# The token norms of an input projection, moved from its input to where its chunks are emptied

## The chip, the cores and the metric

The kernel runs on one core of one Trainium2 chip. The metric is the device time of one execution in microseconds (us): the median over several runs, each on the chip. A separate execution is recorded by the hardware profiler, and all views of the profile come from that one. The engines are named as in the profile: PE is TensorE (PEld its weight loads), DVE is VectorE, ACT is ScalarE, POOL is GpSimd, SP is SyncE, whose queue issues most of the DMAs.

## The reference, cut to what matters

One layer of a streaming encoder over 16 learned meta tokens and 256 tokens of width 2048, everything in float32.

```python
h = concat([meta, x])                                  # 272 tokens x 2048
xn = rmsnorm(h, norm_mix)                              # h * rsqrt(mean(h*h) + eps) * norm_mix
q, f_logit, i_in, g_out, u = split(xn @ w_in)          # 4 x 1024 columns, and 1024 of u
o_hg = hgrn2_mixer(q, f_logit, i_in, g_out, ...)       # 8 heads; silu(q), sigmoid(f), v = i, silu(g)
o_s5 = s5_mixer(u, ...)                                # scan, GELU, GLU with w_glu, norm
h = h + concat([o_hg, o_s5]) @ w_out
h = h + conv_ffn(rmsnorm(h, norm_ffn), w_gate, w_up, conv_w, conv_b, w_down)
out = rmsnorm(h[:, 16:], final_norm)
```

The factor rsqrt(...) of a token is one number for its row of xn, so it is also one number for its row of xn @ w_in. norm_mix is one number for each of the 2048 input channels.

## The kernel before, in words

All weights stream from HBM once, in units of 1 MB (128 partitions x 2048 values, tile `raw`, three buffers). A float32 product is made of three single-pass matmuls: each operand is split into a rounded high part and the rest, and hi\*hi, hi\*lo and lo\*hi are added up in PSUM. For the weights `wsplit` does it: ACT casts a half of a unit (128x1024) to `whi`, and DVE subtracts that from `raw` into `wlo`; three buffers of each. The input of the projection is split the same way into `xh` and `xl`, sixteen K tiles of 128 channels x 272 tokens, with tokens along the free axis. `mm3` (L173) runs over the units, their halves, the two blocks of 128 columns and the four K tiles of a half, with three matmuls each (L187, L188, L189).

`chunk` (L772) computes 256 columns of w_in: two units, two accumulators `acc` of 128x272 (or 258) in the PSUM pool `pmm`, which has three buffers, and 96 matmuls. The twenty chunks run in the order written in `ORDER`: u0, then for h0 the three chunks f, q and i, then u1, h1 and so on to h3, and at the end g0 to g3. Each chunk is emptied at once:

- u: `s5_u` (L560) copies both accumulators into `ysb` on ACT. The S5 part follows (`s5_tile`, `s5_scan`): per chunk eight scans of DVE, ACT and POOL work and small matmuls.
- f: `hg_f` (L639): per accumulator two sigmoids on ACT that read PSUM.
- q and g: `hg_q` (L650) and `hg_g` (L675): a sigmoid on ACT and then a product on DVE, both reading PSUM.
- i: `hg_i` (L658): ACT copies to SBUF, PE transposes, ACT copies the transposes into `v` and `vm`.
- After f, q and i the HGRN2 work of two heads follows (`hg_group`, `hg_cross`), most of it on DVE.

After the twenty chunks come the GLU (its input is split into `gh` and `gl` at L827 and L828), the output projection, the MLP and the down projection, which are not touched.

The start is what the change rewrites. The x rows (tokens on partitions) are loaded in four halves, PE transposes them, and DVE and ACT copy the transposes to `xT` (L311 to L321). `row_rs` (L268) takes a row block's sum of squares, half on ACT (L275) and half on DVE (L276), and `sqrt_rs` (L258) makes the inverse root with five small DVE instructions and one on ACT. `spread` (L290) turns the three columns into a tile `rbs` that has each token's factor on every partition, through PE and PSUM. Ten matmuls into a spare accumulator follow (NWARM2, L305). Then each K tile takes three instructions: DVE `xn` = xT\*gm\*rbs (L333), ACT `xh` (L334), DVE `xl` (L335). The first chunk's two weight units are loaded early (`early`, L247 and L251) and split in halves of 512 columns, where DVE makes the `wlo` of the first quarter of a unit and POOL the other three; one-column copies from `xh` (L160, `deps`) hold these splits back behind certain K tiles.

The instructions are ordered by a planner: each gets a priority from its place in the program, `pri(n)` moves a block forward (negative) or back, and the planner simulates the engines and takes, for each, the ready instruction with the best priority. Weight splits have -4, the emptying -3, HGRN2 work -2, the main matmuls of `mm3` +1. The whole start stands 900000 ahead of everything else. On the chip each engine then runs its instructions in the planned order. `tc.issue_after(i)` puts the instructions of its block behind instruction i on i's engine.

Of the kernel before, what the change touches and what calls it, by code (L numbers as in the profile page):

```python
# [9 lines left out]
F32 = mybir.dt.float32  # L10
# [7 lines left out]
NM = 16  # L18
# [11 lines left out]
T0 = NM - 2  # L30
# [9 lines left out]
NWARM2 = 10  # L40
# [33 lines left out]
def hymba_kernel(ctx: ExitStack, tc: tile.TileContext, x, meta, lb_logits, norm_mix, w_in, hg_norm,  # L74
# [71 lines left out]
    deps = []  # L146

    def wunit(src):
        with pri(-4):
            return wsplit(early.pop(0), (dve, pool), 2, deps.pop(0)) if early else wsplit(wload(src))  # L150

    def wsplit(raw, eng=(dve, dve), parts=1, dep=None):
        res = []
        n = 1024 // parts
        for hf in range(2):
            hi = wsp.tile([128, 1024], F32R, tag="whi", name="whi")
            lo = wsp.tile([128, 1024], F32R, tag="wlo", name="wlo")
            if dep is not None and dep[hf] is not None:

                act.copy(out=hi[:, 0:1], in_=dep[hf])  # L160
            for i in range(parts):
                c = slice(i * n, (i + 1) * n)
                act.copy(out=hi[:, c], in_=raw[:, hf, c])  # L163
                tt(lo[:, c], raw[:, hf, c], hi[:, c].bitcast(F32), SUB, eng[max(hf, i)])
            res.append((hi, lo))
        return res
# [61 lines left out]
    sp.dma_start(out=xm, in_=meta)  # L228
    HD = D // 2
# [12 lines left out]
    for b in range(2):  # L242
        for hf in range(2):
            sp.dma_start(out=xt[b][:, hf * HD:(hf + 1) * HD], in_=x[b * 128:(b + 1) * 128, hf * HD:(hf + 1) * HD])
        if b == 0:
            sp.dma_start(out=nrow, in_=norm_mix.rearrange("o (r c) -> (o r) c", c=128))
# [40 lines left out]
    rbp = [pmm.tile([128, NM + 128], F32, tag="mm", name=f"rbp{b}") for b in range(2)]  # L287
    rbs = xin.tile([128, T], F32, name="rbs")
# [5 lines left out]
    rm = row_rs(xm, NM, 1, "rm")  # L294
    rb = [None, None]
    for b in range(2):
        rb[b] = row_rs(xt[b], 128, 2, f"rb{b}")
        if b == 0:
            spread(rm, NM, rbp[0][:, 0:NM])
            spread(rb[0], 128, rbp[0][:, NM:])  # L300
            act.copy(out=rbs[:, 0:NM + 128], in_=rbp[0])
        else:
            spread(rb[1], 128, rbp[1][:, 0:128])
            dve.tensor_copy(out=rbs[:, NM + 128:T], in_=rbp[1][:, 0:128])
            for _ in range(NWARM2):  # L305
                pe.matmul(wps, ident, rbs[:, NM + 128:T], start=True, stop=True)
        for i in range(4):
            pp, tg = ((pbu, "bu"), (py, "y"), (psc, "sc"), (pbu, "bu"))[i]
            xps = pp.tile([128, 4, 128], F32, tag=tg, name="xps")
            for k in range(4):  # L310
                pe.transpose(xps[:, k], xt[b][:, (4 * i + k) * 128:(4 * i + k + 1) * 128], ident)  # L311
            dst = xT[:, 4 * i:4 * i + 4, NM + 128 * b:NM + 128 * (b + 1)]
            if i % 2:
                act.copy(out=dst, in_=xps)
            else:
                dve.tensor_copy(out=dst, in_=xps)
        if b == 0:
            xps = ptp.tile([128, KD, NM], F32, tag="tp", name="xps")
            for kt in range(KD):
                pe.transpose(xps[:, kt], xm[:, kt * 128:(kt + 1) * 128], ident[0:NM, 0:NM])  # L320
            act.copy(out=xT[:, :, 0:NM], in_=xps)  # L321
            gm = prm.tile([128, KD], F32, name="gm")
            gps = ptp.tile([128, KD], F32, tag="tp", name="gps")
            pe.transpose(gps, nrow, ident[0:KD, 0:KD])
            ts(gm, gps, -0.5, MUL)
# [4 lines left out]
    tc.cur_priority -= 900000  # L330
    for kt in range(KD):
        xn = xin.tile([128, T], F32, tag="xn", name="xn", bufs=4)
        stt(xn, xT[:, kt], gm[:, kt:kt + 1], rbs, MUL, MUL)  # L333
        act.copy(out=xh[:, kt, :], in_=xn)  # L334
# [225 lines left out]
    def s5_u(j, ps):  # L560
        pv = ps.rearrange("p (k s) -> p s k", s=2)
        act.copy(out=ysb[:, j], in_=pv)
# [87 lines left out]
    def hg_q(h0, accs):  # L650
        q = hgp.tile([128, 2, NQ], F32, tag="q", name="q")
        sg = hgp.tile([128, 2, NQ], F32, tag="sg", name="sg")
        for m in range(2):
            fact(sg[:, m], accs[m], AF.Sigmoid)
            stt(q[:, m], accs[m], lbc[:, 1, h0 + m:h0 + m + 1], sg[:, m], MUL, MUL)
        return q

    def hg_i(accs):  # L658
# [8 lines left out]
        act.copy(out=v, in_=tp)  # L667
# [393 lines left out]
```

## Time and profile before

| | |
|---|---|
| median of 3 runs | 1241.25 us (1241.08 to 1242.11) |
| the profiled execution | 1245.4 us, span 1243.6 us |
| PE busy | 1220.0 us (98%) |
| DVE busy | 878.6 us (71%) |
| ACT busy | 605.9 us (49%) |
| POOL busy | 91.1 us (7%) |

The span runs from the first to the last instruction of the profiled execution. Matmuls overlap each other in the record, so a busy PE is not a PE at its peak: how fast it goes is read from the distance between the starts of matmuls and from the granted clock (1.00 is full speed). A view of windows gives, for each stretch, its length, the busy time of each engine with its instructions in brackets, the clock, the busy share of the DMA engines and their GB/s. A row of the timeline has start, duration, engine, line, operation, output<-inputs, shapes and count, and in square brackets the engine's idle time before it and what ended that.

### The profile page before, as it was taken

The numbers are of one execution on the slowest core, as the hardware profiler recorded it, in microseconds if no ns is written. First come the engines' busy times: TensorE is split into PE (matmuls) and PEld (weight loads), VectorE is DVE, ScalarE is ACT, GpSimd is POOL, SyncE is SP. The second block draws the span as 40 slices with busy tenths as digits, with TensorE's granted clock in tenths as the row PEclk, the third lists the DMA queues.
The fourth block names the chain that finished last, engine by engine and source line by source line (L and its number), as shares of the span: only waits on it lengthen the run. The fifth ranks groups of instructions, "written<-read, shape, count | busy, mean of one in ns | idle before, by whom it ended". The sixth has DMA issues, their size and how long they took to land.

```text
span 1243.6 us, 22643 instructions
## 1 busy us (share of the span) xinstructions
PE 1220.0 (98%) x9235; PEld 1146.4 (92%) x9235; DVE 878.6 (71%) x1535; ACT 605.9 (49%) x1054; POOL 91.1 (7%) x116
## 2 busy tenths in 40 slices
PE   7999999999999999999999999999999999999997
PEld 6999998989979999999999999999999988888886
DVE  7899999999977877765656656656656644545554
ACT  6756566675645455433433433434333434444454
POOL 5221211322100000000000000000000000000000
PEclk8999999999999999999999999999999999999999
DMA  8454443334335555565555656555565645555552
GB/s 241 147 149 131 143 142 106 113 109 144 127 102 169 171 178 196 170 195 179 183 190 176 197 171 194 179 184 190 174 199 170 230 165 184 200 201 184 191 208 97
DMA packets 176295, 210.73 MB, mean 169 GB/s; under 512 B 14772, under 2 KB 168879, under 8 KB 170415
## 3 DMA queue, kind: packets, MB, share of 16 engines
q1 hardware_dynamic: 175871, 209.20, 51.8%
q8 instruction: 72, 1.18, 0.4%
q14 instruction: 32, 0.26, 0.1%
q0 software_dynamic: 320, 0.09, 0.0%
HBM read 206.05 MB, written 2.10 MB: 167 GB/s over the span
## 4 chain that ended last, share of the span: by engine, by line
PE 95%; DVE 3%; DMA 1%; issue 0%; ACT 0%; SPq 0%; DVEq 0%; ACTq 0%
PE acc L189 10%; PE acc L188 10%; PE acc L187 9%; PE ua L188 7%; PE ua L187 7%; PE ga L187 7%; PE ua L189 7%; PE ga L189 7%; PE ga L188 7%; PE d L984 6%; PE d L982 6%; PE d L983 6%; PE bu L602 1%; PE lps L731 1%; DVE wlo L85 1%; DVE xn L94 1%
## 5 line engine op out<-in xcount | busy, mean ns | idle before, releaser
L85 DVE TENSOR_TENSOR wlo<-raw,whi 128x1024 fp32r<-128x1024 f32 (+1 forms) x376 | 461.2, 1227 | 305.1 <-ACT whi L163 255.6
L163 ACT CAST whi<-raw 128x1024 fp32r<-128x1024 f32 (+1 forms) x382 | 397.8, 1042 | 517.2 <-PE ga L188 158.2
L187 PE MATMUL ga<-fh,whi 128*128 128x258 f32 x704 | 199.0, 283 | 0.5 <-DVE a L85 0.5
L189 PE MATMUL ga<-fh,wlo 128*128 128x258 f32 x704 | 198.5, 282 | 0.0
L188 PE MATMUL ua<-fl,whi 128*128 128x256 f32 x704 | 198.4, 282 | 0.0
L188 PE MATMUL ga<-fl,whi 128*128 128x258 f32 x704 | 198.1, 281 | 0.0
L189 PE MATMUL ua<-fh,wlo 128*128 128x256 f32 x704 | 197.9, 281 | 0.0
L187 PE MATMUL ua<-fh,whi 128*128 128x256 f32 x704 | 197.9, 281 | 0.0
L188 PE MATMUL acc<-xl,whi 128*128 128x272 f32 (+1 forms) x640 | 186.9, 293 | 2.3 <-DVE xl L85 2.3
L189 PE MATMUL acc<-xh,wlo 128*128 128x272 f32 (+1 forms) x640 | 184.3, 293 | 3.8 <-DVE wlo L85 3.8
L187 PE MATMUL acc<-xh,whi 128*128 128x272 f32 (+1 forms) x640 | 185.9, 294 | 0.0
L187 PEld LDWEIGHTS ga<-fh,whi 128*128 128x128 f32 x704 | 133.0, 189 | 0.7 <-DVE a L85 0.7
L188 PEld LDWEIGHTS ga<-fl,whi 128*128 128x128 f32 x704 | 133.5, 190 | 0.0
L187 PEld LDWEIGHTS ua<-fh,whi 128*128 128x128 f32 x704 | 133.1, 189 | 0.0
L189 PEld LDWEIGHTS ua<-fh,wlo 128*128 128x128 f32 x704 | 132.9, 189 | 0.0
L188 PEld LDWEIGHTS ua<-fl,whi 128*128 128x128 f32 x704 | 132.8, 189 | 0.0
L189 PEld LDWEIGHTS ga<-fh,wlo 128*128 128x128 f32 x704 | 132.6, 188 | 0.0
L982 PE MATMUL d<-whi,ah 128*128 128x512 f32 x328 | 127.7, 389 | 0.0
L188 PEld LDWEIGHTS acc<-xl,whi 128*128 128x128 f32 x640 | 121.8, 190 | 6.4 <-DVE xl L85 3.2
L983 PE MATMUL d<-whi,al 128*128 128x512 f32 x328 | 127.6, 389 | 0.0
L189 PEld LDWEIGHTS acc<-xh,wlo 128*128 128x128 f32 x640 | 120.9, 191 | 6.7 <-DVE wlo L85 4.3
L187 PEld LDWEIGHTS acc<-xh,whi 128*128 128x128 f32 x640 | 121.1, 190 | 3.3 <-issue 1.7
(381 smaller groups left out, 1840.3 us busy)
## 6 DMA issues: line engine op xcount, KB each, us to landing
raw<-in_w_ffn_gate SPq DMA_DIRECT2D x44, 1024.0 KB, 5.1
raw<-in_w_ffn_up SPq DMA_DIRECT2D x44, 1024.0 KB, 5.1
raw<-in_w_ffn_down SPq DMA_DIRECT2D x44, 1024.0 KB, 4.8
raw<-in_w_in SPq DMA_DIRECT2D x39, 1024.0 KB, 5.2
raw<-in_w_out SPq DMA_DIRECT2D x16, 1024.0 KB, 5.4
raw<-in_w_glu SPq DMA_DIRECT2D x4, 1024.0 KB, 5.2
x<-in_x SPq DMA_DIRECT2D x4, 512.0 KB, 5.9
out<-ob SPq DMA_DIRECT2D x8, 256.0 KB, 2.8
```

Of the source, the lines that this page charges most:

```text
L85: eng.tensor_tensor(out=dst, in0=a, in1=b, op=op)
L94: dve.scalar_tensor_tensor(out=dst, in0=a, scalar=s, in1=b, op0=op0, op1=op1, **kw)
L163: act.copy(out=hi[:, c], in_=raw[:, hf, c])
L187: pe.matmul(accs[m], lh, xh[:, n0:n1], start=first, stop=False)
L188: pe.matmul(accs[m], lh, xl[:, n0:n1], start=False, stop=False)
L189: pe.matmul(accs[m], ll, xh[:, n0:n1], start=False, stop=end)
L602: return pe.matmul(bus[i][:, ri], bt[h, 2 * ri + q0 // 2], R[h, q0 // 2], start=True, stop=True)
L731: pe.matmul(ps[:, i], kt[:, i], qf[:, 64 * i:64 * (i + 1)], start=True, stop=True)
L982: pe.matmul(dps[t][n], ah[:, tk], hi, start=False, stop=False, skip_group_check=True)
L983: pe.matmul(dps[t][n], al[:, tk], hi, start=False, stop=False, skip_group_check=True)
L984: pe.matmul(dps[t][n], ah[:, tk], lo, start=False, stop=end, skip_group_check=True)
```

## The change

The K tiles of the projection's input no longer contain the tokens' factors: `xh` and `xl` are the split of xT\*gm. The twenty chunks therefore come out without the tokens' factors, and these are multiplied in where a chunk is emptied.

```diff
 # the start
+    sp.dma_start(out=nrow, in_=norm_mix...)            # now right behind meta, ahead of x
-        if b == 0:
-            sp.dma_start(out=nrow, in_=norm_mix...)
...
-    def wsplit(raw, eng=(dve, dve), parts=1, dep=None):
+    def wsplit(raw):                                   # whole halves, wlo always on DVE
...
-    rbp = [pmm.tile([128, NM + 128], F32, tag="mm", name=f"rbp{b}") for b in range(2)]
-    rm = row_rs(xm, NM, 1, "rm")
+    pe.transpose(gps, nrow, ident[0:KD, 0:KD]); dve.tensor_copy(out=gm, in_=gps)
     for b in range(2):
-        rb[b] = row_rs(xt[b], 128, 2, f"rb{b}")
-        ... spread, copies into rbs, NWARM2 matmuls
         ... transposes of x and copies into xT, as before
+    last = None
+    for p in range(8):                                 # eighths of the first chunk's two units
+        u, hf, c = p // 4, p // 2 % 2, slice(512 * (p % 2), 512 * (p % 2) + 512)
+        hi, lo = units[u][hf]
+        raw = early[u][:, hf, c]
+        def split():
+            i = act.copy(out=hi[:, c], in_=raw)
+            tt(lo[:, c], raw, hi[:, c].bitcast(F32), SUB)
+            return i.ins
+        with tc.issue_after(last):                     # from p = 1 on
+            wi = split()
+        with tc.issue_after(wi):
+            for kt in (2 * p, 2 * p + 1):
+                last = act.activation(out=xh[:, kt], in_=xT[:, kt], func=AF.Identity, scale=gm[:, kt:kt + 1]).ins
+                stt(xl[:, kt], xT[:, kt], gm[:, kt:kt + 1], xh[:, kt].bitcast(F32), MUL, SUB)
+    rcol = s5p.tile([128, 3], F32, name="rcol")
+    rb = [row_rs(xt[0], 128, 2, "rb0")]
+    with pri(0.5):
+        rb += [row_rs(xt[1], 128, 2, "rb1"), row_rs(xm, NM, 1, "rm")]
+    for i, n in enumerate((128, 128, NM)):
+        ts(rcol[:n, i:i + 1], rb[i], -0.5, MUL)
-    for kt in range(KD):
-        stt(xn, xT[:, kt], gm[:, kt:kt + 1], rbs, MUL, MUL)
-        act.copy(out=xh[:, kt, :], in_=xn)
-        tt(xl[:, kt, :], xn, xh[:, kt, :].bitcast(F32), SUB)
 # the emptying of chunks
     def s5_u(j, ps):
-        act.copy(out=ysb[:, j], in_=pv)
+        tt(ysb[:, j], pv, rv, MUL)                     # rv: rbs in the same order
     def hg_f(h0, accs):
-            fact(k[:, m], accs[m], AF.Sigmoid, scale=-1.0)
-            fact(f[:, m], accs[m], AF.Sigmoid)
+            tt(f[:, m], accs[m], rbs, MUL)
+        fact(k, f, AF.Sigmoid, scale=-1.0)
+        fact(f, f, AF.Sigmoid)
     def hg_q(h0, accs):
-            fact(sg[:, m], accs[m], AF.Sigmoid)
-            stt(q[:, m], accs[m], lbc[...], sg[:, m], MUL, MUL)
+            tt(q[:, m], accs[m], rbs[:, T0:T], MUL)
+        fact(sg, q, AF.Sigmoid)
+            stt(q[:, m], q[:, m], lbc[...], sg[:, m], MUL, MUL)
     def hg_i(accs):                                    # tokens lie on partitions here
-        act.copy(out=v, in_=tp)
+        for b in range(2):
+            fact(v[... b], tp[... b], AF.Copy, scale=rcol[:, b:b + 1])
-        act.copy(out=vm, in_=tp[0:NM, 0:2])
+        fact(vm, tp[0:NM, 0:2], AF.Copy, scale=rcol[0:NM, 2:3])
     def hg_g(h0, accs):
-            fact(sg[:, m], accs[m], AF.Sigmoid)
-            stt(gs[:, h0 + m], accs[m], vcol[...], sg[:, m], MUL, MUL)
+            tt(gs[:, h0 + m], accs[m], rbs[:, T0:T], MUL)
+            fact(sg[:, m], gs[:, h0 + m], AF.Sigmoid)
+            stt(gs[:, h0 + m], gs[:, h0 + m], vcol[...], sg[:, m], MUL, MUL)
     def do_u(c):
         accs = chunk(w_in, 16 + c)
+        if c == 0:                                     # rbs is made behind the first chunk
+            rbp = pmm.tile([128, T], F32, tag="mm", name="rbp")
+            spread(rcol[0:NM, 2:3], NM, rbp[:, 0:NM])
+            for b in range(2):
+                spread(rcol[:, b:b + 1], 128, rbp[:, NM + 128 * b:NM + 128 * (b + 1)])
+            act.copy(out=rbs, in_=rbp)
```

More of the change, by code (lines that the diff above doesn't have):

```diff
@@ L39 @@
 NWARM = 8
-NWARM2 = 10
 LATE = 1.003
@@ L157, in wsplit @@
             lo = wsp.tile([128, 1024], F32R, tag="wlo", name="wlo")
[L158 to L164, printed above, removed]
+            act.copy(out=hi, in_=raw[:, hf])
+            tt(lo, raw[:, hf], hi.bitcast(F32), SUB)
             res.append((hi, lo))
@@ L228, in hymba_kernel @@
     sp.dma_start(out=xm, in_=meta)
+    sp.dma_start(out=nrow, in_=norm_mix.rearrange("o (r c) -> (o r) c", c=128))
     HD = D // 2
@@ L286, in hymba_kernel @@
         pe.matmul(wps, ident, ident, start=True, stop=True)
-    rbp = [pmm.tile([128, NM + 128], F32, tag="mm", name=f"rbp{b}") for b in range(2)]
-    rbs = xin.tile([128, T], F32, name="rbs")
+    rbs = s5p.tile([128, T], F32, name="rbs")
     def spread(r, n, ps):
         pe.matmul(ps, r.to_broadcast([n, 128]), ident[0:n, 0:n], start=True, stop=True)
-    rm = row_rs(xm, NM, 1, "rm")
-    rb = [None, None]
+    gm = prm.tile([128, KD], F32, name="gm")
+    gps = ptp.tile([128, KD], F32, tag="tp", name="gps")
+    pe.transpose(gps, nrow, ident[0:KD, 0:KD])
+    dve.tensor_copy(out=gm, in_=gps)
     for b in range(2):
-        rb[b] = row_rs(xt[b], 128, 2, f"rb{b}")
[L298 to L306, printed above, removed]
         for i in range(4):
@@ L321, in hymba_kernel @@
             act.copy(out=xT[:, :, 0:NM], in_=xps)
[L322 to L325, printed above, removed]
+    last = None
+    for p in range(8):
+        u, hf, c = p // 4, p // 2 % 2, slice(512 * (p % 2), 512 * (p % 2) + 512)
+        if p % 4 == 0:
+            units.append([])
+        if p % 2 == 0:
+            units[u].append([wsp.tile([128, 1024], F32R, tag=t, name=t) for t in ("whi", "wlo")])
+        hi, lo = units[u][hf]
[4 more added lines that the diff above has]
+            return i.ins
+        if last is None:
+            wi = split()
+        else:
+            with tc.issue_after(last):
+                wi = split()
+        with tc.issue_after(wi):
[8 more added lines that the diff above has]
+        ts(rcol[:n, i:i + 1], rb[i], -0.5, MUL)
     tc.cur_priority += 900000
     pool.memset(ones, 1.0)
-    tc.cur_priority -= 900000
-    for kt in range(KD):
-        xn = xin.tile([128, T], F32, tag="xn", name="xn", bufs=4)
-        stt(xn, xT[:, kt], gm[:, kt:kt + 1], rbs, MUL, MUL)
-        act.copy(out=xh[:, kt, :], in_=xn)
-        tt(xl[:, kt, :], xn, xh[:, kt, :].bitcast(F32), SUB)
-    tc.cur_priority += 900000
-    deps[:] = [(None, xh[:, 0, 0:1].bitcast(F32)), tuple(xh[:, i, 0:1].bitcast(F32) for i in (3, 6))]
     vps = ptp.tile([128, 100], F32, tag="tp", name="vps")
@@ L560, in s5_u @@
     def s5_u(j, ps):
-        pv = ps.rearrange("p (k s) -> p s k", s=2)
-        act.copy(out=ysb[:, j], in_=pv)
+        pv, rv = (a.rearrange("p (k s) -> p s k", s=2) for a in (ps, rbs))
+        tt(ysb[:, j], pv, rv, MUL)
     def s5_split(j):
@@ L642, in hg_f @@
         for m in range(2):
+            tt(f[:, m], accs[m], rbs, MUL)
+        fact(k, f, AF.Sigmoid, scale=-1.0)
+        fact(f, f, AF.Sigmoid)
+        for m in range(2):
             h = h0 + m
-            fact(k[:, m], accs[m], AF.Sigmoid, scale=-1.0)
-            fact(f[:, m], accs[m], AF.Sigmoid)
             fact(f[:, m], f[:, m], AF.Identity, scale=lbc[:, 1, h:h + 1], bias=lbc[:, 0, h:h + 1])
@@ L653, in hg_q @@
         for m in range(2):
-            fact(sg[:, m], accs[m], AF.Sigmoid)
-            stt(q[:, m], accs[m], lbc[:, 1, h0 + m:h0 + m + 1], sg[:, m], MUL, MUL)
+            tt(q[:, m], accs[m], rbs[:, T0:T], MUL)
+        fact(sg, q, AF.Sigmoid)
+        for m in range(2):
+            stt(q[:, m], q[:, m], lbc[:, 1, h0 + m:h0 + m + 1], sg[:, m], MUL, MUL)
         return q
```

10 lines of the change are left out of this document (5 added, 5 removed).

## The prediction, made before the changed kernel was run

> **What bounds the kernel now.** I read the page's totals, then busy times by stage, then the timeline of the start, then the waits of the stage of the twenty chunks.
>
> ```profile
> PE 1220.0 (98%) x9235; PEld 1146.4 (92%) x9235; DVE 878.6 (71%) x1535; ACT 605.9 (49%) x1054; POOL 91.1 (7%) x116
> ```
>
> ```profile
> core 0: us, PE busy (x) PEld busy (x) DVE busy (x) ACT busy (x) POOL busy (x), PEclk, DMA share, GB/s
> 13.00:21.00 8.00, 6.52 (x31) 5.66 (x31) 7.29 (x18) 6.22 (x16) 2.98 (x3) 0.57 1.13 324
> 34.00:60.00 26.00, 26.00 (x214) 26.00 (x213) 23.05 (x99) 18.64 (x37) 6.08 (x12) 1.00 0.47 139
> 60.00:345.00 285.00, 281.20 (x2452) 258.72 (x2452) 272.79 (x560) 177.93 (x471) 66.14 (x76) 0.99 0.42 130
> 370.00:1000.00 630.00, 628.87 (x5215) 625.21 (x5215) 411.15 (x620) 266.35 (x328) 0.00 (x0) 1.00 0.57 183
> ```
>
> PE is the bound, and from 370 us on it alone: DVE is busy 411 of 630 us there, and nothing of the change lies there. From 60 to 345 us both are full: PE 281.2 and DVE 272.8 of 285 us. So an instruction added to DVE in that stage is not hidden by a glance at DVE's 71%. What is left is the start:
>
> ```profile
> 21.07 0.30 PEld L187 LDWEIGHTS acc<-xh,whi 128*128 128x128 f32 x2
> 25.37 0.29 PE L187 MATMUL acc<-xh,whi 128*128 128x272 f32 x1
> 25.50 0.29 PE L188 MATMUL acc<-xl,whi 128*128 128x272 f32 x1
> 29.61 0.39 PE L188 MATMUL acc<-xl,whi 128*128 128x272 f32 x1 [1.76 <-DVE xl L85]
> 31.18 0.43 PE L189 MATMUL acc<-xh,wlo 128*128 128x272 f32 x1
> 31.41 0.43 PE L188 MATMUL acc<-xl,whi 128*128 128x272 f32 x1
> ```
>
> ```profile
> 17.00:21.00 4.00, 4.00 (x21) 0.56 1.15 325
> 21.00:24.00 3.00, 2.85 (x24) 1.00 0.80 133
> 31.00:34.00 3.00, 3.00 (x14) 0.50 0.92 316
> 21.00:34.00 13.00, 10.49 (x63) 0.87 0.64 184
> ```
>
> The first real matmul starts at 21.07 us. At full clock they start 0.126 us apart (25.37 and 25.50; over longer stretches 0.126), at half clock 0.23 us (31.18 and 31.41, the window of clock 0.50). The last row is that of the tile `acc` alone: 63 matmuls in the 13 us to 34 us, where 103 would fit. The starved PE waits for DVE, which works off `xn` and `xl`. From 34 us on PE runs without a gap. So at 34.0 us the main work done is 63 x 0.126 = 7.9 us, and **26.1 us are lost** at the start.
>
> **The change part by part: the start.** Which steps stand there now:
>
> ```profile
> 12.89 1.12 ACT L163 CAST whi<-raw 128x512 fp32r<-128x512 f32 x2
> 13.68 0.69 DVE L85 TENSOR_TENSOR wlo<-raw,whi 128x512 fp32r<-128x512 f32 x1
> 14.28 1.22 DVE L94 SCALAR_TENSOR_TENSOR rb1y<-rb1t,rb1y 128x1 f32<-128x1 f32 x1
> 17.75 1.74 DVE L94 SCALAR_TENSOR_TENSOR xn<-xT,gm,rbs 128x272 f32<-128x272 f32 x4
> 18.28 0.83 ACT L334 CAST xh<-xn 128x272 fp32r<-128x272 f32 x2 [0.45 <-DVE xn L94]
> 25.85 3.41 POOL L85 TENSOR_TENSOR wlo<-raw,whi 128x512 fp32r<-128x512 f32 x2 [2.30 <-ACT whi L163]
> 26.61 1.53 DVE L94 SCALAR_TENSOR_TENSOR xn<-xT,gm,rbs 128x272 f32<-128x272 f32 x1
> ```
>
> The first quarter of weights is there at 12.89 us (ACT casts it then). The x rows are there before (11.20, ACT's wait for the last of them; the row above it is that of the spare matmuls):
>
> ```profile
> 17.35 3.88 PE L306 MATMUL wps<-rbs,ident 128*128 128x128 f32 x19
> 11.20 0.63 ACT L82 ACTIVATE junk<-x 128x512 bf16<-128x512 f32 x1 [0.63 <-DMA x<-in_x]
> L94 DVE SCALAR_TENSOR_TENSOR junk<-x x4: 670/689/693, 6.0 to 11.7; 128x512 bf16<-128x512 f32 x4
> 8.52 3.92 SPq L142 DMA_DIRECT2D raw<-in_w_in  x2
> DMA to landing us min/median/max: 5.3/9.5/11.3
> ```
>
> Between 12.89 and 21.07 us lie the row sums, roots, `rbs`, the last transposes behind them, `gm` and `xn`. All but the transposes, their copies and `gm` leave this path. What remains: cast 0.56 us (1.12 for two), two `xh` of 0.42, so the first matmul can start at 12.9 + 0.56 + 0.42 = 13.9 us; I take 14.3 for hand-overs. If the planner leaves sums of squares ahead of the cast on ACT (four of 0.63 us), it is up to 17.
>
> Then each of the eight steps needs on DVE one `wlo` quarter of 0.62 us (0.69 less the 0.07 by which neighbours overlap in the record) and two `xl` as scalar_tensor_tensor of 0.41 (priced by `xn`: 1.74 us for four, less overlap): 1.44 us. On ACT 0.56 + 2 x 0.41 = 1.38, and on PE twelve matmuls of 0.126 = 1.51 us. So PE paces the steps, by a hair. The 16 `xn` go, and with POOL's six `wlo` goes what they did to DVE: a one-column product took 1.22 us and an `xn` 1.53 us beside POOL's. DVE takes over those six quarters (3.7 us, inside the 1.44 per step).
>
> The ten NWARM2 matmuls go, so the first matmuls meet the clock of an idle PE, 0.57 between 13 and 21 us. Bounds: none, if the transposes keep it up, or some 3.4 us at half clock (steady spare matmuls began at 17.35, and the clock is 0.56 up to 21 us and 1.00 from there), which loses 1.7 us. I take 1.6, the nearest row being that window.
>
> By the Trainium skill ("TensorE: Matmul & The Clock Gate", Part 1) PE's clock is at half by default and full after about 3.4 us of sustained activity, which would make that loss an estimated 1.7 us; the trace agrees for the way up. For the way down the page wants an idle window of about 3.4 us. There the trace differs: the wait of 1.76 us before 29.61 was followed by 0.50 from 31 to 34 us, so I price each PE wait of about 2 us at double.
>
> Lost at the start after: 14.3 + 1.6 + 0.5 for steps not met exactly = 16.4 us. **PE's lead is 26.1 - 16.4 = 9.7 us**; with a first matmul at 17 us it is 7.
>
> Costed at nothing: norm_mix's DMA ahead of x on SP's queue (one 0.43 us issue, x was waited for in 11.20 already, but 14.3 does not hang on it); the second unit's arrival, issued at 8.52 plus 9.5 = 18.0 us, against step five at 14.3 + 4 x 1.51 = 20.3; POOL's queue keeps its loads.
>
> **The emptying.** Added to DVE: 2 products per chunk of u, f, q and g, 32 in all, one operand in PSUM. The nearest row is the MLP's:
>
> ```profile
> L85 DVE TENSOR_TENSOR a<-ga,rsb x44: 416/419/426, 514.3 to 980.6; 128x258 f32<-128x258 f32 x44
> L562 ACT COPY ysb<-acc x8: 368/387/394, 41.4 to 240.5; 128x272 f32<-128x272 f32 x8
> DVE wlo L85 <- ACT whi L163: 7.7, 13, 2.4
> DVE rhv L91 <- PE hps L857: 3.1, 1, 3.1
> PE acc L189 <- DVE wlo L85: 3.8, 2, 2.1
> 345.00:364.00 19.00, 16.71 (x137) 12.97 (x135) 13.89 (x27) 9.52 (x20) 0.77 (x1) 1.00 0.32 106
> ```
>
> 32 x 0.35 to 0.42 = 11.2 to 13.4 us; I take 12. ACT loses eight copies of 0.39, merges sigmoids and gains four scalings; it has room (178 of 285 us) and is costed at nothing. The products of q and g with their sigmoids now read SBUF: same length.
>
> Does DVE hold that? From 34 to 364 us (when it splits the GLU's input) it is busy 23.05 + 272.79 + 13.89 = 309.7 of 330 us, so 20.3 idle. After: its steps run from about 13.5 for 8 x 1.44 = 11.5 us, to 25.0; of the row sums (four of 0.69, meta's of 1.2 and some 2.5 of small ones, 6.5 us) most fit into the wait before 13.5, and I leave 2 us: 27. Then 27 + 309.7 + 12 = 348.7 us plus idle time. With all 20.3 idle it ends at 369, 5 us later than now; with 6 at 354.7, which is PE's lead. 7.7 of the idle time is DVE waiting for a cast that waits for PE to free its buffer, and 3.1 waiting for PE's `hps`: both shrink when PE is ahead. Less these two it is 9.5, and I take 10.3: DVE ends at 359, **5 us earlier** than now. So of PE's lead of 9.7 us, DVE lets through 5, and what is late next is DVE's S5 work ahead of the GLU.
>
> Emptying also moves: an accumulator is now freed by one DVE product, where u and f took ACT, and q and g a sigmoid and a DVE product. `pmm` has three buffers, so the next chunk has 12 matmuls (1.5 us) before it needs one more. The first time there is no spare one, since `rbs` sits in it: row sums, three spreads, a copy and a product come before h0's first matmul. With sums done by 27 us and u0 finished at 14.3 + 1.6 + 12.1 + 0.5 = 28.5, I cost that at nothing; if all 6.5 us come after 25.0, `rbs` is there at about 33, a wait of 4 us.
>
> Sum: span 1243.6 - 5 = 1238.6 us. The profiled execution took 1245.4, 1.8 more than its span and 4.15 above the median, so against the median: 1241.25 - 5 = **1236.2 us**.
>
> **The rivals.** A: DVE absorbs all. Its idle time falls to 6 us or its S5 tail slips behind the GLU's first splits; PE's lead comes through, 1241.25 - 9.7 = 1231.6, and down to 1229.5 if the two waits for `wlo` (3.8 us, with their clock) go too. For it: most of DVE's waits are waits for a lagging PE. Against: 98% of busy time from in-order instructions is rare; it has 95.7% in the stage now.
>
> B: DVE takes it all back. With 13 to 18 us of idle time, against 20.3 now, it ends within 2.5 us of 364 (348.7 + 15.3 in the middle), and PE waits ahead of the GLU longer than now: 1241 us. For it: 12 us more of DVE work in a stage where DVE is full. This is also the case in which the change doesn't do what it says, with the start given back.
>
> C: the slower side: PE waits for its accumulators. Every chunk but i is emptied behind what DVE has in hand:
>
> ```profile
> 198.04 3.34 DVE L704 RECIPROCAL rv<-SP 128x512 f32<-128x512 f32 x1
> 202.51 0.39 PE L189 MATMUL acc<-xh,wlo 128*128 128x272 f32 x1 [1.70 <-DVE wlo L85]
> 362.80 0.51 PE L187 MATMUL acc<-gh,whi 128*128 128x258 f32 x2 [1.60 <-ACT gh L827]
> 364.21 0.39 PE L187 MATMUL acc<-gh,whi 128*128 128x258 f32 x1 [0.91 <-DVE gs L94]
> ```
>
> A reciprocal of 3.34 us outlasts the 1.5 us of cover, and did so with a `wlo`. 9.7 us spread over 16 chunks is 0.6 each: above that mean wait it decides. At 0.85 us it is 13.6 - 9.7 = 4 us slower: 1245. Against it: q and g let go after one DVE instruction instead of two in a row, and the planner places the emptying ahead of everything but splits; only one such wait (0.91) shows now.
>
> **How the numbers follow.** No change can be told from one within 0.2% (2.5 us: 1238.8 to 1243.7). Forecast 0.40 (its own range 1233 to 1238.8), A 0.25, B 0.15, C 0.20. Faster is forecast plus A, 0.65; same 0.15; slower 0.20. The range reaches from A's low end, 1229.5, to C's 1245; some 0.03 lies below and 0.12 above.
>
> **What would show it.** First real matmul at 13.9 to 17 us, with half clock for about 3 us; chunk u0 done near 28.5 instead of some 38 (34.0 and 33 more matmuls); DVE products on `acc` of 0.42 us, 32 in all; no POOL `wlo`. DVE over 96% busy between 40 and 340 us, and the GLU's first matmul near 357 instead of 362.8. The rest must keep its length. I would be wrong if `rbs` came late, if the planner set the row sums ahead of the casts, or if waits for `acc` or `wlo` multiplied in the stage.

## The result, and the profile after

The changed kernel took 1249.87 us (median of 4 runs, 1248.84 to 1250.94) against 1241.68 us for the kernel before (4 runs, 1241.08 to 1242.24): a ratio of 1.006 (95% interval 1.004 to 1.0079), 8 us slower where 5 us faster was forecast. Its profiled execution took 1250.04 us with a span of 1248.3 us, so that one stands at its median; the profiled execution of before (1245.4 us) stands 3.7 us above its own, so the two profiles lie 4.6 us apart and not 8.

Totals and stages of the changed kernel, in the columns of before:

```profile
PE 1217.7 (98%) x9215; PEld 1144.8 (92%) x9215; DVE 882.1 (71%) x1559; ACT 605.0 (48%) x1035; POOL 93.0 (7%) x110
```

```profile
13.00:21.00 8.00, 6.20 (x28) 5.74 (x29) 8.00 (x22) 8.00 (x20) 1.95 (x4) 0.61 1.14 327
34.00:60.00 26.00, 26.00 (x217) 25.74 (x216) 23.96 (x95) 18.70 (x32) 7.72 (x12) 1.00 0.57 175
60.00:345.00 285.00, 282.14 (x2433) 259.87 (x2431) 271.42 (x562) 172.00 (x443) 70.94 (x69) 0.99 0.42 133
345.00:370.00 25.00, 11.50 (x102) 6.60 (x102) 23.93 (x59) 10.57 (x33) 3.24 (x3) 0.72 0.05 18
370.00:1000.00 630.00, 629.00 (x5219) 626.83 (x5220) 412.53 (x622) 268.62 (x332) 0.00 (x0) 0.99 0.56 183
```

The row to look at is 345 to 370 us: PE is busy 11.5 of 25 us, DVE 23.9. Before, PE had 16.71 of 19 us between 345 and 364. In the long stretch from 60 to 345 us DVE is no fuller than before (271.42 against 272.79 of 285 us), although 30 products of 0.41 to 0.43 us now lie between 34 us and the end of the stage. Here they are, in the view of DVE's groups there; the two of u0 come before 34 us:

```profile
L84 DVE TENSOR_TENSOR gs<-acc,rbs 128x258 f32<-128x258 f32 x8 | 3.3, 416 | 0.4 <-PE acc L182 0.4
L84 DVE TENSOR_TENSOR q<-acc,rbs 128x258 f32<-128x258 f32 x8 | 3.3, 413 | 0.4 <-PE acc L182 0.4
L84 DVE TENSOR_TENSOR PP<-acc,rbs 128x272 f32<-128x272 f32 x8 | 3.2, 429 | 0.0
L84 DVE TENSOR_TENSOR ysb<-acc,rbs 128x272 f32<-128x272 f32 x6 | 2.6, 432 | 0.0
```

So 12.4 us of products went in, and what they pushed out is seen at the end of the stage. Timeline of PE, then of DVE, then the long row of PE's waits over the whole execution:

```profile
344.41 0.29 PE L181 MATMUL acc<-xl,whi 128*128 128x258 f32 x1
344.54 0.28 PE L182 MATMUL acc<-xh,wlo 128*128 128x258 f32 x1
...
351.95 0.50 PE L616 MATMUL yps<-ysb,k 128*128 128x136 f32 x2
...
363.85 1.13 PE L620 MATMUL yps<-xo,cp 128*32 128x136 f32 x16 [11.40 <-DVE xo L84]
...
369.72 1.01 PE L180 MATMUL acc<-gh,whi 128*128 128x258 f32 x3 [0.32 <-ACT gh L844]
```

```profile
361.39 0.75 DVE L592 TENSOR_TENSOR_SCAN m<-r,m 128x136 f32<-128x136 f32 x2
362.08 0.39 DVE L84 TENSOR_TENSOR rht<-rhy 8x258 f32<-8x258 f32 x1
362.40 0.71 DVE L84 TENSOR_TENSOR P<-W,m 128x544 f32<-128x544 f32 x1
363.03 0.41 DVE L93 SCALAR_TENSOR_TENSOR rht<-rhv,rht 8x258 f32<-8x258 f32 x1
363.37 0.42 DVE L84 TENSOR_TENSOR xo<-P 128x272 f32<-128x272 f32 x1
...
369.92 0.42 DVE L84 TENSOR_TENSOR gh<-ysb,gh 128x258 fp32r<-128x258 f32 x1
```

```profile
PE yps L620 <- DVE xo L84: 11.4, 1, 11.4
```

PE is done with the chunks at 344.8 us (before, their last matmul starts at 360.92). After some small matmuls of S5 and the HGRN2 norm, the next thing in its order is the S5 part's last output `yps`, for which it waits 11.4 us on DVE's last `xo`. DVE works back to back: S5's last scans, and between them the HGRN2 norm's chain (`rht`, `rhy`), which the GLU does not need. After that `xo` it goes on in the same way: the GELU of the last `yps` shares DVE with more of the norm until `gh` is cast at 369.25 us. The GLU's first matmul starts at 369.72 us, 6.9 us later than before (362.80). The start, in contrast, began when it was forecast to. PE's timeline, and below it the window of the tile `acc` alone, of before and of after:

```profile
14.37 0.52 PE L180 MATMUL acc<-xh,whi 128*128 128x272 f32 x2 [0.73 <-ACT xh L329]
...
15.96 0.59 PE L181 MATMUL acc<-xl,whi 128*128 128x272 f32 x1 [1.07 <-DVE xl L93]
16.35 0.43 PE L182 MATMUL acc<-xh,wlo 128*128 128x272 f32 x1
16.58 0.43 PE L180 MATMUL acc<-xh,whi 128*128 128x272 f32 x1
...
21.56 0.33 PE L181 MATMUL acc<-xl,whi 128*128 128x272 f32 x1
21.73 0.29 PE L182 MATMUL acc<-xh,wlo 128*128 128x272 f32 x1
21.85 0.29 PE L180 MATMUL acc<-xh,whi 128*128 128x272 f32 x1
```

```profile
13.00:34.00 21.00, 10.49 (x63) 9.58 (x64) 0.00 (x0) 0.00 (x0) 0.76 0.83 237
```

```profile
13.00:34.00 21.00, 17.65 (x113) 16.93 (x114) 0.88 (x2) 0.00 (x0) 0.84 0.86 242
```

At 34.0 us PE has 113 main matmuls behind it instead of 63: 50 x 0.126 = 6.3 us of lead. None of it is left behind the wait for `xo`.

### The profile page after: what moved, and what is told of

Its sections match the earlier page's. It is cut to its first block, busy times and chain, and to the rows that moved or that the text cites. A ratio compares the mean times of both kernels' runs of the same rounds, so it can differ in the third digit from the quotient of the medians.

```text
span 1248.3 us, 22606 instructions
## 1 busy us (share of the span) xinstructions
PE 1217.7 (98%) x9215; PEld 1144.8 (92%) x9215; DVE 882.1 (71%) x1559; ACT 605.0 (48%) x1035; POOL 93.0 (7%) x110
## 4 chain that ended last, share of the span: by engine, by line
PE 95%; DVE 3%; ACT 1%; DMA 1%; issue 0%; SPq 0%; DVEq 0%; ACTq 0%
PE acc L181 10%; PE acc L182 10%; PE acc L180 10%; PE ua L181 7%; PE ua L180 7%; PE ga L180 7%; PE ua L182 7%; PE ga L182 7%; PE ga L181 7%; PE d L1000 6%; PE d L999 6%; PE d L1001 6%; PE bu L606 1%; PE lps L742 1%; DMA x<-in_x 1%; PE lps L737 0%
## 5 line engine op out<-in xcount | busy, mean ns | idle before, releaser
L156 ACT CAST whi<-raw 128x1024 fp32r<-128x1024 f32 x374 | 393.9, 1054 | 545.4 <-PE ga L181 158.1
```

Source lines behind the costliest of these rows:

```text
L156: act.copy(out=hi, in_=raw[:, hf])
```

## The experiments

Four theories. **D**: the sum of DVE's work up to the GLU sets the GLU's start, and the products use up what room there was. **S**: the new start, or the new plan that comes with it, costs the time. **T**: what costs is the order at the end, where the norm's chain lies between S5's scans. **C**: accumulators come free too late (the prediction's third rival), above all behind long DVE instructions.

All runs in one table. "DVE busy" is its busy time from 34 us to the GLU's first matmul, "idle" the rest of that stretch. "Ratio" is to the kernel before in the same batch (medians of 1241.7 to 1243.0 us). The last three columns are from the profiled execution, the time is a median.

| kernel | us | ratio (95%) | GLU starts | DVE busy | idle |
|---|---|---|---|---|---|
| before | 1241.68 | | 362.80 | 308.5 | 20.3 |
| after | 1249.87 | 1.006 (1.004 to 1.0079) | 369.72 | 319.0 | 16.7 |
| e1 after, no products | 1236.27 | 0.9944 (0.993 to 0.9959) | 356.11 | 303.8 | 18.3 |
| e2 before, with products | 1248.52 | 1.0045 (1.003 to 1.006) | 368.82 | 324.2 | 10.6 |
| e12 after, half the products | 1238.44 | 0.9967 (0.9958 to 0.9976) | 357.76 | 308.5 | 15.3 |
| e9 after, no reciprocals | 1234.74 | 0.9938 (0.9923 to 0.9953) | 354.63 | 298.5 | 22.1 |
| e3 after, norm's priority 0 | 1248.45 | 1.0048 (1.0029 to 1.0067) | 369.21 | 319.1 | 16.1 |
| e4 before, norm's priority 0 | 1238.86 | 0.9969 (0.9957 to 0.9982) | 357.96 | 306.2 | 17.7 |
| e5 after, norm behind the GLU's split | 1246.61 | 1.0035 (1.0021 to 1.0048) | 366.14 | 312.7 | 19.5 |
| c1 before, planned anew | 1243.36 | 1.0012 (1.0003 to 1.0022) | 362.62 | 309.2 | 19.4 |
| c2 after, planned anew | 1245.74 | 1.0023 (1.0014 to 1.0033) | 367.17 | 314.4 | 18.8 |
| e15 before, the split in turn alone | 1244.42 | 1.0013 (1.0004 to 1.0022) | 363.94 | 308.2 | 21.7 |
| e6 after, products on POOL | 1241.10 | 0.9986 (0.9974 to 0.9997) | 362.15 | 320.1 | 8.0 |
| e14 after, f and q on POOL, priority 0 | 1247.00 | 1.003 (1.002 to 1.004) | 366.40 | 318.9 | 13.6 |
| e7 norms in the transposes | 1251.11 | 1.0076 (1.0057 to 1.0095) | 365.38 | 318.5 | 12.9 |
| e8 rows scaled first | 1243.23 | 1.0009 (0.9997 to 1.002) | 362.50 | 315.2 | 13.4 |
| e8b the same, norm's priority 0 | 1244.35 | 1.0014 (1.0005 to 1.0023) | 364.13 | 317.3 | 12.8 |

In the profiled executions the time less the GLU's start is 879 to 883 us for all 17: behind the GLU little changes, and where the GLU starts decides. (The profiled execution stands 3.7 us above the median in before, 3.0 in e6 and 5.0 below it in e7.)

"DVE busy" and "idle" add up to the GLU's start by definition, so the table shows how much each moved and not which one caused it. Load alone does not fix the start: in after, e3, e6, e7 and e14 DVE is busy 318.5 to 320.1 us, and the GLU starts anywhere from 362.15 to 369.72 us, since the idle time is 8.0 to 16.7. D says in which direction work on DVE moves the end. The rest goes with the order of the plan, as far as the runs below can tell, and is not shown.

**e1, the new start without the products.** In `s5_u`, `hg_f`, `hg_q` and `hg_g` the emptying of before is put back, and `rbs` is not made. This kernel leaves out the tokens' factors of u, f, q and g:

```diff
-        tt(ysb[:, j], pv, rv, MUL)
+        act.copy(out=ysb[:, j], in_=pv)
...
-            tt(q[:, m], accs[m], rbs[:, T0:T], MUL)
```

> The changed kernel with the chunks emptied as before: the tokens' factors of u, f, q and g are left out (32 DVE products fewer), everything else of the change stays. Theory D (the products fill up DVE, which then sets when the S5 work ends and PE can begin the GLU): the first GLU matmul moves from 369.7 us to 353 to 357 us and the time falls to about 1233 us (1230 to 1237). Theory S (the new start or the new plan is at fault, not the products): 1246 to 1250 us. Theory T (the order at the end of the stage: the HGRN2 norm runs ahead of the last S5 scans on DVE): 1246 to 1250 us, since that order stays.

1236.27 us, 6.5 below the kernel before in its batch. S is refuted: without the products the new start gains. That the gain resembles the changed kernel's lead of 6.3 us is chance: e1 itself has 128 main matmuls behind it at 34 us, a lead of 8.2 us, because PE's clock rose earlier in this execution. Not all of it came out, since PE waits 3.9 us for `gh` ahead of the GLU, where it waited 1.6 before. The window at the end of the stage has PE busy 21 of 25 us again; the second row is that wait:

```profile
345.00:370.00 25.00, 21.13 (x175) 19.67 (x174) 18.86 (x40) 13.21 (x27) 0.00 (x0) 0.93 0.39 125
PE acc L180 <- ACT gh L833: 3.9, 1, 3.9
```

**e2, the old start with products.** The emptying of the changed kernel, by a tile of ones:

```diff
+    rb1 = s5p.tile([128, T], F32, name="rb1")
+    pool.memset(rb1, 1.0)
...
+            tt(f[:, m], accs[m], rb1, MUL)
```

> The kernel before with the 32 products added in the emptying, by a tile of ones; its start stays. D: DVE ends some 8 to 12 us later and PE waits ahead of the GLU: 1250 to 1256 us. S: 1241 to 1243 us. T: 1243 to 1246 us.

1248.52 us, 5.8 above before (D's range began at 1250), and the wait of the changed kernel is there without its start:

```profile
PE yps L619 <- DVE xo L85: 8.4, 1, 8.4
```

So the products alone cost 5.8 us and the start alone gains 6.5, and together they cost 8.2 (3.5 in c2, the same kernel planned anew). They don't add: with the products DVE ends last, and PE's lead turns into a longer wait, 11.4 us in place of 8.4.

**e12, half of the products** (those of f and q left out, u and g kept; the edit is that of e1 for these two).

> The changed kernel without the products of f and q (16 of the 32 left out, 6.7 us of DVE). D: about half of the 13.6 us that all 32 cost: 1241 to 1245 us. A loss through the plan alone would not go by halves.

1238.44 us, below the forecast of 1241 to 1245: it does not go by halves. With 0, 16 and 32 products the time is 1236.3, 1238.4 and 1249.9 us: the first half costs 2.2 us of its 6.7 us of DVE work, the second 11.4 (7.3 if c2 below stands for all 32). A bound that is met on the way looks like this, and a fixed cost per product would not; but the two halves differ by 5 to 9 us, and a new plan alone moved the changed kernel by 4, so the shape is a hint. Part of it is the HGRN2 norm, of which 3.4 us of DVE's instructions stand ahead of the GLU here and 8.3 in the changed kernel (more under e5).

**e9, other work off DVE.** The four reciprocals of 128x512, 3.34 us each, are replaced by ACT copies, so this kernel leaves the inverses out:

```diff
-        dve.reciprocal(out=rv, in_=SP[:, :, NM:T])
+        act.copy(out=rv, in_=SP[:, :, NM:T])
```

> The changed kernel with the four reciprocals of the HGRN2 part (3.34 us each on DVE, 13.4 us in all) left out, an ACT copy in their place; the 32 products stay. D (it is the sum of DVE's work in the stage that counts, wherever it stands): as without the products, 1235 to 1239 us. C (it is the place of the products, at the accumulators): 1247 to 1250 us.

1234.74 us with all 32 products kept: 13.4 us off DVE took 15 us off the time. DVE's busy time ahead of the GLU fell by more, 20.5 us, since most of the norm's chain came behind the GLU's start as well. This tells D from C and from a story about the emptying itself. No matmul of the chunks waits for a product in the changed kernel either; the view of PE's waits from 34 to 345 us lists two, both in the i chunks:

```profile
PE vtp L673 <- ACT iv L669: 1.9, 1, 1.9
PE vtp L680 <- ACT v L81: 0.9, 1, 0.9
```

**e3 and e4, the norm's priority.** One edit, in the changed kernel and in the kernel before:

```diff
-    with pri(-2):
+    with pri(0):
```

> The changed kernel with the HGRN2 norm planned behind the S5 work (priority 0 in place of -2). D alone: the norm's DVE work of some 6 to 8 us moves behind the start of the GLU, which begins near 363: 1242 to 1245 us. T: the whole lead of PE comes out, GLU near 354, 1234 to 1238 us. S: 1249 to 1250 us.

> The kernel before with the same move of the HGRN2 norm. D and T: the wait ahead of the GLU (2.5 us, with a slow clock behind it of about 2 us) goes: 1237 to 1240 us. S: 1241 us, as before.

In the changed kernel it is worth 1.4 us at most (1248.45, where D and T had 1245 or less; the wait for `xo` is still 10.4). The edit did not do what it was meant to: the planner fills what it takes for gaps with the norm's chain all the same, and DVE's instructions of that chain ahead of the GLU add up to 8.3 us as before the edit. In the kernel before it gained some 4 us: 1238.86, and the view of waits lists none of the GLU's first matmul at 357.96. This is the fastest kernel here that does all of the work. But the edit took only 0.8 us of the chain (2.6 to 1.8) from ahead of the GLU there, and in e8b below the same edit gains nothing, so most of the 4 us may be the plan's luck.

**e5, the norm's chain held back.** `tc.issue_after` puts it behind the split of the GLU's input on DVE:

```diff
-    with pri(-2):
+    with tc.issue_after(glast):      # the last gl subtraction
```

> The changed kernel with the HGRN2 norm's DVE work held back behind the split of the GLU's input (an edge in the plan, since priority 0 still let it fill gaps). D: some 6 us of DVE work leave the last stretch, the GLU starts near 364 in place of 369.7, unless the norm then comes too late for the output projection: 1243 to 1246 us. T (the tail's order is the cause): 1236 to 1240 us.

1246.61 us; the wait for `xo` shrinks from 11.4 to 6.1 us, and 3.0 of waiting for `gh` appear. These are rows of the chain in the changed kernel, in the view of DVE's groups from 34 us to the GLU's first matmul:

```profile
L93 DVE SCALAR_TENSOR_TENSOR rhy<-rht,rhy 8x258 f32<-8x258 f32 x3 | 1.8, 599 | 0.0
L84 DVE TENSOR_TENSOR oT<-oT,bps 128x258 f32<-128x258 f32 x3 | 1.3, 419 | 0.1
L84 DVE TENSOR_TENSOR ml<-oT,mh 128x258 fp32r<-128x258 f32 x2 | 0.9, 429 | 0.3
```

With the other rows of `rhv`, `rht`, `rhy` and `hr` the chain has 18 instructions of 8.3 us there. Ahead of the GLU of the kernel before stand 7 of them (2.6 us), in e2 6.9 us, in e1 4.7, in e5 none. In these kernels a late S5 part goes with more of the norm in front of the GLU. T is a part of the loss, 3.3 of 8 us (itself no more than a new plan can move), and not its cause: e5 has nothing of the chain ahead of the GLU and e1 has 4.7 us, and still e5 is 10 us slower.

**c1 and c2, a plan made anew** (one spare matmul more at the start, NWARM 9 for 8, in before and after).

> A control: the kernel before with nine warm-up matmuls at the very start in place of eight, which does no work on the path but makes the planner order everything anew. By every theory the time should stay near 1242; what it moves is the size of a difference that a new plan alone can make. I expect less than 3 us.

> The same control for the changed kernel: D expects 1247 to 1252 us (the DVE work is the same in any order); if the new plan was the cause of the loss, it could fall back to 1242 us or below.

The kernel before moves by 1 us, the changed one by 4 (1245.74), and stays slower than before (1.0014 to 1.0033). So about 4 us of the changed kernel's time are chance of its plan, and differences of that size between two kernels here show nothing by themselves. D's 1247 to 1252 for c2 was missed by a little. The control was also less empty than it was meant to be: in c2 PE's clock was 1.00 from 13 to 34 us (0.84 in after), with 134 main matmuls behind it at 34 us in place of 113. That is 2.6 us more of lead, and PE still waits 11.1 us for `xo`. Ahead of the GLU c2 has the same 712 DVE instructions as after, and they are busy 4.6 us less, because the same forms took less time each; why is not shown.

**e15, the other half of the change alone.** The first weights split in turn with the K tiles, all `wlo` on DVE, the norms left in `xn`.

> The kernel before with the other half of the change alone: the norms stay in xn at the start, nothing is multiplied where chunks are emptied, but the first weights are split in eighths in turn with the K tiles that meet them, all wlo on DVE, and the one-column holds are gone. By theory D no work is added to DVE in the stage but six quarter wlo of 0.62 at the start (3.7 us), less POOL's hold on DVE there: the time is that of the kernel before within some 2 us, 1240 to 1244, the first matmul at 20 to 22 us, the GLU's first matmul at 361 to 365. If the split in turns itself were what cost the changed kernel its 8 us: 1247 or more with a wait of PE's yps.

1244.42 us, 1.7 above before, GLU at 363.94, no wait for `yps`: as D has it. The first matmul came at 17.98 us, earlier than forecast, and 93 stood behind PE at 34 us, but ahead of the GLU PE waited 3.8 us for `gh`. This half costs nothing that exceeds 2 us, and its lead gains nothing by itself.

**e6, the products on POOL.** ACT copies the accumulator out of PSUM, POOL multiplies in SBUF; 20 POOL instructions, two accumulators in one for f, q and g:

```diff
-            tt(f[:, m], accs[m], rbs, MUL)
+            act.copy(out=f[:, m], in_=accs[m])
+        tt(f, f, rbs.unsqueeze(1).to_broadcast([128, 2, T]), MUL, pool)
```

> The changed kernel with the 32 products moved from DVE to POOL, behind an ACT copy out of PSUM (20 larger instructions on POOL). D: 13 us leave DVE: 1236 to 1241 us; if POOL's work holds DVE up as in the start of the kernel before (an xn of 0.42 us took 1.53 us beside it), up to 1248. C (PE waits for accumulators that DVE frees late): about 1249 us less those waits, of which the trace shows under 1 us, so 1248 us.

1241.10 us: 9 us better than the changed kernel, and within 0.2% of the kernel before. DVE lost 32 products and was no less busy than with them: 320.1 us against 319.0 in the changed kernel, and 303.8 in e1, which has nine DVE instructions fewer up to the GLU. That the GLU starts 7.6 us earlier than in the changed kernel at the same load is idle time, 8.0 us in place of 16.7, and D does not explain it. The same forms took longer than in e1, here two of DVE's groups in e1 and then in e6 (60 to 345 us):

```profile
L84 DVE TENSOR_TENSOR wlo<-raw,whi 128x1024 fp32r<-128x1024 f32 x66 | 81.7, 1238 | 7.8 <-ACT whi L156 6.1 <-ACT sq L81 1.3
L84 DVE TENSOR_TENSOR xo<-P 128x272 f32<-128x272 f32 x32 | 14.4, 450 | 0.1
```

```profile
L84 DVE TENSOR_TENSOR wlo<-raw,whi 128x1024 fp32r<-128x1024 f32 x67 | 81.7, 1220 | 0.3 <-ACT whi L156 0.2
L84 DVE TENSOR_TENSOR xo<-P 128x272 f32<-128x272 f32 x30 | 17.5, 582 | 0.0
```

`xo` went from 450 to 582 ns; over all forms that both have the growth is some 9 us in this window. The Trainium skill ("Perfetto Trace Analysis", "Optimizing Scalar/DVE Operations") says that POOL and DVE share a read port, so that moving work between them might not help. The trace agrees for `xo` (+29%), not for `wlo` (1238 to 1220 ns), and it shows durations only, not the port.

**e14, half of the products on POOL** (f and q as in e6, u and g on DVE, the norm's priority as in e3).

> The changed kernel with the products of f and q (16 of 32) made as an ACT copy out of PSUM and one POOL multiply per chunk (8 POOL instructions), u and g left on DVE, and the HGRN2 norm's priority at 0 instead of -2. Theory D (the sum of DVE's work in the stage of the chunks sets the GLU's start): DVE loses 16 x 0.42 = 6.7 us, which brought 1238.4 with these products left out, and gets back part of it from POOL's work beside it (20 POOL multiplies made DVE 8 us busier, so 8 of them some 3): 1239 to 1243, and 1236 to 1240 if the norm's priority is worth here what it was in the kernel before (3). DVE busy 274 to 277 of 285 us from 60 to 345; the GLU's first matmul at 358 to 363. Rival (POOL makes DVE as much busier as it takes off): 1245 to 1250, GLU at 366 or later.

1247.00 us: the rival's answer. POOL is 14 us busier than in e12, DVE 10 us (318.9 against 308.5) and not the 3 that I took from e6. From 60 to 345 us DVE is busy 274.3 us, as D had it; the surplus lies at the end. The wait for `xo` is back at 11.4 us. Half of the 10 us is the norm's chain, 8.3 us of it ahead of the GLU against 3.4 in e12, for all its priority of 0. The rest goes with the same forms taking longer, 3.6 us from 60 to 345 us. Why these 8 multiplies hurt more than e6's 20 is not settled. The late first matmul (16.70 us, 14.13 in e12) is not it: at 34 us both have as many behind them, 116 and 114.

**e7, e8 and e8b, the factors on x's rows.** e7 multiplies by a diagonal matrix where x is transposed:

```diff
-                pe.transpose(xps[:, k], xt[b][...], ident)
+                pe.matmul(xps[:, k], xt[b][...], dg[b], start=True, stop=True)   # dg: diagonal of the factors
```

> A version of mine: the start in steps as in the changed kernel, but the token factors are put into the transposes of x (PE multiplies by a diagonal matrix in place of the identity), so that no chunk needs a product; the residual is multiplied back before the output projection (16 products of 0.42 us and a reciprocal, in a stage where DVE is busy 65%). D: the first matmul at 15.5 to 17 us instead of 14.4, and else as without the products: 1236 to 1239 us. S (the stepwise start is at fault): 1246 to 1250 us.

e8 scales the rows in SBUF in quarters, on DVE and ACT in turn, and then transposes; e8b is e8 with the norm's priority 0.

> As the version with the factors in the transposes, but the x rows themselves are scaled in SBUF (DVE and ACT, quarters of a row block of 0.4 to 0.6 us each) and transposed with the identity as before, since the true float32 products cost PE 0.37 us each in the start and held the first matmul until 25.9 us. D: first matmul at 15.5 to 17 us, no products at the chunks: 1236 to 1239 us. S: 1246 to 1250 us.

> The same with the HGRN2 norm at priority 0, which took about 3 us from the kernel before: 1233 to 1237 us by D; no change against the version without it if that gain was the plan's luck.

Misses, all three: the chunks need no products, but the lead is gone too. In e7 the first matmul came at 25.89 us, since the float32 matmuls that stand for transposes waited 6.07 us for the roots and then took 5.89 us for the first sixteen (two records each):

```profile
12.70 5.89 PE L307 MATMUL xps<-dg,x 128*128 128x128 f32 x32 [6.07 <-DVE rb1y L93]
...
18.52 3.74 PE L299 MATMUL xps<-dg,xm 16*128 16x16 f32 x32
...
22.19 3.84 PE L307 MATMUL xps<-dg,x 128*128 128x128 f32 x32
```

In e8 it came at 19.84, in e8b at 21.58. The factors ahead of the transposes put the roots back on the path from which the change had taken them. And a part of the products is back: the 16 products and the reciprocal for the residual, which the expectation put into a stage where DVE has room, were planned into the full one (in e8 from 84.9 us to 100.4 us, 7.5 us of DVE). DVE is busy 315.2 us up to the GLU in e8, against 303.8 in e1. e8b, meant to show whether e4's gain was luck, is 1.1 us slower than e8: by its own expectation, luck, as far as one kernel can tell.

**e10, e11 and e13, the reciprocals on POOL** as a power of -1 (after, before, and after with the norm's priority 0):

```diff
-        dve.reciprocal(out=rv, in_=SP[:, :, NM:T])
+        tt(rv, SP[:, :, NM:T], neg1.unsqueeze(1).to_broadcast([128, 2, 256]), ALU.pow, pool)
```

> The changed kernel with DVE's four reciprocals done by POOL (a power of -1), result intact. D: 13.4 us leave DVE as in the run without reciprocals (1234.7): 1235 to 1240 us, if POOL's power takes under about 8 us each and holds DVE up little; up to 1246 if it is slow, since the HGRN2 chain waits for it.

> The kernel before with the same move. D: PE is its bound there and waits for DVE in few places (1.6 + 0.9 us ahead of the GLU, 3.8 us for weights), so the same 13.4 us off DVE are worth only 3 to 7 us: 1235 to 1239. If the work on DVE were the bound in both kernels alike, 1228 to 1230.

> The changed kernel with the reciprocals on POOL and the HGRN2 norm at priority 0. D: with DVE relieved PE is the bound, and the norm's move is worth what the GLU still waits, 0 to 3 us: 1233 to 1238 us. A version that should beat both kernels.

1453.31, 1479.05 and 1453.16 us: they tell nothing on D, since POOL needs 82 us for each, and PE waits for the result:

```profile
L84 POOL TENSOR_TENSOR rv<-SP,neg 128x512 f32<-128x512 f32 x4 | 329.6, 82405 | 27.5 <-DVE SP L84 15.6 <-DVE W L93 7.0 <-DVE pw L88 5.0
```

```profile
PE dps L723 <- DVE qt L84: 138.2, 4, 45.4
```

## Why the prediction was wrong, point by point

**The step that failed: "Does DVE hold that?"** It asked for the right thing and answered it with too little idle time. It had DVE's end at 27 + 309.7 + 12 plus idle time, and took 10.3 us of it where 20.3 stand before. The form was right: it took the later of two ends, DVE's at 359 us against PE's at 354.3. DVE's end came at 369.7. The measured rows, before and after, from 34 us to the GLU's first matmul:

```profile
34.00:362.80 328.80, 323.40 (x2798) 297.40 (x2796) 308.54 (x682) 204.89 (x522) 73.00 (x88) 0.99 0.41 128
```

```profile
34.00:369.72 335.72, 319.36 (x2748) 291.93 (x2746) 319.03 (x712) 200.99 (x506) 81.90 (x84) 0.97 0.41 128
```

Idle: 335.7 - 319.0 = 16.7 us, 6.4 more than taken. Work: in the prediction DVE had 7 us of the stage behind it at 34 us, so 309.7 + 12 - 7 = 314.7 us to go; it had 319.0, 4.3 more. The 4.3 is a balance. From 27 to 34 us DVE did 2.5 us less than taken, since it was idle for 2.0 (its window, below) and the last `xl` of the start ended at 27.5. Another 5.7 us of the norm's chain stand ahead of the GLU than before (8.3 against 2.6, under e5), a shift that the prediction did not think of. Against these, what before still did of the start behind 34 us is gone (the last `xl` and `xn`, 2.6 us), and smaller items. 6.4 + 4.3 = 10.7 us, which is 369.7 against the 359 forecast.

Rival B was the nearest. Its idle time, 13 to 18 us, holds the measured 16.7, and what it lacked is the work: 348.7 + 16.7 is 365.4 and not 369.7. The prediction's own bound, "With all 20.3 idle it ends at 369", has the measured end by luck: too much idle time by 3.6 and too little work by 4.3.

Why the idle time stayed is in the reason given for its shrinking: "7.7 of the idle time is DVE waiting for a cast that waits for PE to free its buffer". With PE ahead these waits should go. The 7.7 is also a row from 60 to 345 us; in the stretch of the 20.3 it is 9.7. In the changed kernel's waits from 34 us to the GLU it has shrunk by 2.2 us only. The wait for `hps` did go, but another of 2.4 us stands there now, for ACT:

```profile
DVE wlo L85 <- ACT whi L163: 9.7, 17, 2.4
DVE wlo L84 <- ACT whi L156: 7.5, 13, 1.4
DVE P L84 <- ACT W L81: 2.4, 3, 1.4
```

The first row is before, the other two are after. Why the casts stay late is not shown; a lead shifts the whole stream of weights, and ACT's casts wait for PE's buffers longer than before, 66.0 us against 43.7 in the same stretch.

DVE's idle time gave way to added work only in part. Over the 17 kernels of the table it falls by some 0.45 us for each us of load, with a wide scatter (8.0 to 16.7 at about 319); the prediction let it fall by 10 for 12.

```profile
27.00:34.00 7.00, 7.00 (x58) 6.90 (x57) 4.97 (x18) 3.63 (x5) 0.00 (x0) 1.00 0.50 156
```

**None of the lead came through.** "So of PE's lead of 9.7 us, DVE lets through 5": e2 shows that with the products DVE ends last even without a lead, so the lead's size doesn't matter. That after (1249.87) is no faster than e2 (1248.52), though it has less DVE work, lies within the 4 us of a plan and is not settled.

**PE's lead was mis-sized** (6.3 us instead of 9.7). The first matmul came at 14.37, 14.3 forecast. But the granted clock stayed at 0.50 until 21.6 us: matmuls 0.23 us apart at 16.35 and 16.58, 0.126 only from 21.73 on. From 16.35 on PE ran without a gap, so full clock came after 5.2 us; I had taken 3.4 us and 1.6 of loss. In fine windows of the traces the clock is low from 14.8 to 21.6 us here, from 13.7 to 20.5 in before, from 16.2 to 19.6 in e1, which has the same steps, and not at all in c2: 6.8 us, 3.4 or none. The Trainium skill ("TensorE: Matmul & The Clock Gate", Part 1) says that the window that sets the clock has about 3.4 us and is free-running, and that the transition varies by some 500 ns for that. The 3.4 us agree with one such window; 6.8 us is as long as two, more than those 500 ns, and the prediction had read it as one. Lost at the start: 34.0 - 113 x 0.126 = 19.8 us, against 16.4.

The loss before was mis-sized too. The clock was 0.76 there from 13 to 34 us. e2 and e4 leave the start as it is, had 1.00, their first main matmul at 18.64 and 18.77 us, and 75 and 74 of them by 34 us in place of 63. So about 1.4 of the 26.1 us belong to the profiled execution, which is some 4 us above the median from which the forecast took its 5 us. On its own a lead of 6.3 us would have left the forecast as it was, since DVE was to let through 5.

**What held.** The products' price (0.41 to 0.43 us against 0.35 to 0.42). `rbs` late: nothing; the first `ysb` product waited for PE's matmul and not for `rbs`:

```profile
31.56 0.44 DVE L84 TENSOR_TENSOR ysb<-acc,rbs 128x272 f32<-128x272 f32 x1 [0.20 <-PE acc L182]
```

Rival C, accumulators freed late: not seen. "What is late next is DVE's S5 work ahead of the GLU": the place was right, and the sign of what it leaves was not. And one sign by which to see it failed plainly: DVE over 96% between 40 and 340 us. It was 95.5% there, and 95.4% before. Here the added work did not fill DVE's gaps but went past the end of the stage. That is not a limit of DVE: in e6 it was busy 97.5% of the time from 34 us to the GLU.

## What to carry to other kernels

Where two engines are both over 95% busy in a stage, the stage ends at the later of their two ends, and a gain on one doesn't pay for a cost on the other: add the new work to the second engine with most of its idle time left in, and compare the two ends. Work taken off the start of such a stage and put back as many small instructions in its middle is paid by the engine that is full; make the gain first (here 6 us, e1) and then look for a place where its price is really free. Look what lies between the last instructions ahead of a hand-over that does not belong there (the norm's chain: 3.3 us in e5), and check where the planner really put what an edit moved: in e3 and in e7 and e8 it was not where the edit meant it to be. Plan a kernel anew before believing a difference of 4 us.

## What the runs showed of the hardware that was not expected

- POOL's `pow` on 128x512 float32 took 82.4 us, some 25 times DVE's reciprocal of the same shape (3.34 us).
- True float32 matmuls of 128x128 took 0.24 us each at a granted clock of 1.00 (e7, 3.84 us for sixteen), about twice a pass of 0.126 us with 272 columns, and 0.37 at 0.63 right behind a wait of PE (5.89); the small ones of 16 rows took 0.23 at 1.00.
- With POOL's multiplies in SBUF beside them (e6) DVE's `xo` took 29% longer on average than in e1, and `wlo` no longer.
- PE's granted clock stayed at 0.50 for 6.8 us in the start of the changed kernel and of before, for 3.4 in e1 and not at all in c2. With 113, 128 and 134 main matmuls done by 34 us, the same steps differ by up to 2.6 us, for the most part through the clock.
